# Three kinds of multiplication moved from VectorE to GpSimd in a two-layer hybrid decoder

## The chip, the cores and the metric

The kernel runs on one core of a Trainium2 chip. The metric is the device time of one execution in microseconds (us). The engines are TensorE (PE in the profile, its weight loads PEld), VectorE (DVE), ScalarE (ACT), GpSimd (POOL) and SyncE (SP), whose queue issues the loads of weights. Each engine works through its own queue in order, and semaphores order the engines among each other.

## What is computed

Two layers on an input of 256 positions by 2048 features, float32:

```
h = rmsnorm(x);  z = h @ w_in                      # [q | k | v | u | gate_attn | gate_ssm]
g_attn, g_ssm = sigmoid(z_gates + gate_bias)
y_attn = sliding_window_attention(q, k, v)         # 16 heads, window 128
y_ssm  = glu(gelu(s5_ssm(u)))                      # 64 groups, a scan over the positions
merged = g_attn * (y_attn @ w_attn_branch) + g_ssm * (y_ssm @ w_ssm_branch)
x = x + merged @ w_out
x = x + (silu(h2 @ w_gate) * (h2 @ w_up)) @ w_ffn_out     # h2 = rmsnorm(x)
```

## The kernel before

The layout is transposed: features lie on the 128 partitions and the 256 positions on the free axis. A projection is worked in slabs of 256 output features; a slab is a row of pieces of 512 input rows (four for `w_in` with its 2048 rows, two for the attention branch with its 1024). For accuracy each piece of weights is split in two: ACT casts the high half (`Weights.high`, L106), DVE subtracts to get the low half (`Weights.low`, L121, 128x1024), and PE multiplies both (L295): the high half with 512 columns, the low one with 256. Two accumulators in PSUM rotate, so a slab can begin only when the slab before the last one has been read out. There are four buffers for each of the raw, high and low pieces.

A slab is read out by `whole` (L340): ACT copies one half of the accumulator into a buffer `wh` (tag `t2`, seven rotate; L343), and DVE adds the other half from PSUM (L344). Because the norm's gain is in the input and its root mean square is not, the sum is then multiplied by `rms` (a 128x256 tile repeated over the slab's two halves).

The order is written by hand: a counter ticks once per piece, `later(n, f)` runs `f` in the program n pieces later, and `stages(n, gen)` runs a generator's next step at each further piece. A layer's slabs run in this order: the inputs of the states (u), k and v, q, then eight slabs of the attention branch's gate (`ga`, L898), eight of the attention branch itself (L918), eight of the states' gate (`gs`, L945), the gated linear unit, the states' branch with the merge (L1026, L1027), `w_out`, and the feed-forward part. Beside them run, a few instructions per piece: the attention of eight pairs of heads (`attend`: the score pass L853 on DVE, exponentials on ACT, transposes L874 and products L848, L885 on PE), beside the slabs of q and `ga`; and the scan of the states (`scan`, L768 and L771: two products and four additions per step on DVE, 127 steps a layer), from the slabs of u to the middle of those of `gs`. The scan's end is waited for by PE's read-out of the states (L965).

The gate of the attention branch goes through a sigmoid on ACT in place (L363, from two pieces after the last `ga` slab), and the branch's slabs are multiplied into it (L918). The states' gate goes through its sigmoid on ACT right after its multiplication (L945). `c_matrices` (L925) fills two tiles with zeros on POOL (L929, L930) and has ACT copy into them (L935), three pieces after the last slab of the branch. Otherwise POOL has only memsets and constants.

Of the kernel before, what the change touches and what calls it, by code (L numbers as in the profile page):

```python
# [135 lines left out]
class Clock:  # L136
# [6 lines left out]
    def later(self, n, fn, *args):  # L143
        self.jobs.setdefault(self.now + max(n, 1), []).append((fn, args))

    def stages(self, n, gen, step=1):


        def go():
            if next(gen, "end") != "end":  # L150
                self.later(step, go)

        if n > 0:
            self.later(n, go)
        else:
            go()
# [11 lines left out]
def build(ctx, tc, a, out):  # L168
    nc = tc.nc
    v, s, g, pe = nc.vector, nc.scalar, nc.gpsimd, nc.tensor  # L170
# [16 lines left out]
    def p8(x, shape, dt=F32):  # L187
        return big.tile(shape, dt, name=nm(x), tag="p8", bufs=8)
# [4 lines left out]
    def t2(x, shape=None, dt=F32):  # L193
        return tmp.tile(shape or [P, 2, T], dt, name=nm(x), tag="t2", bufs=7)
# [5 lines left out]
    later, stages = ck.later, ck.stages  # L200
# [107 lines left out]
    def slab(key, rhs, wide):  # L308
        for ps in products(key, rhs, wide):
            pass  # L310
        return ps
# [28 lines left out]
    def whole(ps, x="wh"):  # L340

        t = t2(x)
        s.copy(t, ps[:, :, T:])  # L343
        v.tensor_add(t, t, ps[:, :, :T])  # L344
        return t

    def over(r):
        return r.unsqueeze(1).to_broadcast([P, 2, T])
# [12 lines left out]
    def sigmoid(o, i, **kw):  # L361
        tables("sigmoid_and_others")
        s.activation(o, i, AF.Sigmoid, **kw)  # L363
# [342 lines left out]
    def layer(l, norm):  # L706
        last_layer = l == L - 1
        rms = norm.r
# [44 lines left out]
        for i in range(4):  # L753
            wide = l > 0 or i > 0
            ps = slab((l, "in", 6 + i), norm.rhs, wide)
# [67 lines left out]
        ps = slab((l, "in", 4), norm.rhs, True)  # L823
        stages(1, normed(kt, ps, qkg[:, l, 1:2]))
        ps = slab((l, "in", 5), norm.rhs, True)
# [63 lines left out]
        for i in range(4):  # L889
            ps = slab((l, "in", i), norm.rhs, True)  # L890
# [4 lines left out]
        ga = []  # L895

        def evict_ga(i, ps):
            v.tensor_mul(ga[i // 4][:, 2 * (i % 4) : 2 * (i % 4) + 2, :], whole(ps), over(rms))  # L898

        for i in range(8):  # L900
            if i % 4 == 0:
                ga.append(p8("ga", [P, 8, T]))
            ps = slab((l, "in", 10 + i), norm.rhs, True)
            later(1, evict_ga, i, ps)
# [10 lines left out]

        def evict_ab(i, ps):
            t = ga[i // 4][:, 2 * (i % 4) : 2 * (i % 4) + 2, :]
            v.tensor_mul(t, t, whole(ps))  # L918

        for i in range(8):  # L920
            ps = slab((l, "ab", i), lambda k: ya[k // 4][:, k % 4, :, :], True)
            later(1, evict_ab, i, ps)
# [19 lines left out]

        def evict_gs(i, ps):
            t = whole(ps, "gs")
            v.tensor_mul(t, t, over(rms))  # L945
            for r in range(2):
                sigmoid(gs[i // 4][:, 2 * (i % 4) + r, :], t[:, r, :], bias=gate_b[:, l, 16 + 2 * i + r : 17 + 2 * i + r])

# [49 lines left out]
        for i in range(8):  # L998
            if i % 4 == 0:
                gs.append(p8("gs", [P, 8, T]))  # L1000
            ps = slab((l, "in", 18 + i), norm.rhs, True)
            later(1, evict_gs, i, ps)


        yg, y = hold["yg"], hold["y"]
# [10 lines left out]
        for i in range(4):  # L1016
            ps = slab((l, "glu", i), lambda k: yg[:, 0, k, :, :], True)
# [13 lines left out]
        for i in range(2, 8):  # L1031
            ps = slab((l, "sb", i), lambda k: yg[:, 1, k, :, :], True)
# [10 lines left out]
        def x_tile(i):  # L1043
            return xn[i // 4][:, 2 * (i % 4) : 2 * (i % 4) + 2, :]

        for i in range(8):
            xo = t2("xo")
            nc.sync.dma_start(xo, src[:, 2 * i : 2 * i + 2, :])
            ps = slab((l, "o", i), lambda k: mg[:, k, :, :], True)
            t = x_tile(i)  # L1050
# [27 lines left out]
        for part, nf in enumerate(FPARTS):  # L1078
            hid = [p8("hid", [P, 4, 2, T], F32R) for _ in range(nf // 4)]
            for i in range(nf // 2):  # L1080
                ps = slab((l, "fg", f0 // 2 + i), norm2.rhs, True)
                stages(3 if part == 0 and i == 0 else 1, gate(ps, i))
                ps = slab((l, "fu", f0 // 2 + i), norm2.rhs, True)
# [14 lines left out]
            for i in range(8):  # L1098
# [3 lines left out]
                ps = slab((l, "fo", part, i), hrhs, True)  # L1102
                t = x_tile(i)
# [17 lines left out]
    for l in range(L):  # L1121
        norm = layer(l, norm)
# [61 lines left out]
```

## Time and profile before

| | |
|---|---|
| median of 3 runs | 2625.94 us (2624.06 to 2626.17) |
| the profiled execution | 2625.52 us, its span 2623.70 us |
| mean granted clock of TensorE | 0.997 of full speed |
| PE, DVE, ACT, POOL busy | 99%, 73%, 48%, 1% of the span |

The busy shares are averages over stages that differ, and PE's ends are modelled, so they are read together with the views by stretch, the waits and the chain of work that ended last. That chain is followed back from the last instruction, at each step to what released it or to the instruction before it on its engine.

### The profile page before, as it was taken

The page shows a single profiled execution, that of the slowest core. Times are in us where ns is not written, and L with a number is a line of the kernel's source. Part 1 is how long each engine was busy: PE and PEld are TensorE (multiplying, and loading weights), DVE is VectorE, ACT ScalarE, POOL GpSimd, SP SyncE. Part 2 cuts the span into 40 slices and gives each one's busy share as a digit, 9 for nine tenths or more (in the row PEclk, how much of TensorE's full clock was granted, in tenths as well). Part 3 has the DMA queues.
Part 4 walks back from the last instruction along what each step waited for, and adds up shares of the span by engine and source line. Part 5 has one row for each costly group of instructions (what it writes and reads, how often), then busy time and mean ns, then how long its engine had stood idle before and what let it go on. Part 6 is the DMA issues. An engine that isn't in the chain of part 4 may idle for free.

```text
span 2623.7 us, 40564 instructions
## 1 busy us (share of the span) xinstructions
PE 2586.1 (99%) x15716; PEld 2254.0 (86%) x15716; DVE 1927.0 (73%) x3655; ACT 1267.4 (48%) x1725; POOL 18.9 (1%) x27
## 2 busy tenths in 40 slices
PE   8999899999999999999999999999999999999999
PEld 7878778888888888888888788888888888888888
DVE  8889997866865666566677999887766656665664
ACT  6566546544443444344455675464544334433442
POOL 1000000000000000000000000000000000000000
PEclk9999999999999999999999999999999999999999
DMA  6534554666655565555664445556666556655655
GB/s 220 177 113 145 155 171 157 205 212 194 200 169 193 194 191 178 191 192 186 204 206 148 137 156 171 177 177 211 208 186 190 181 197 191 188 190 185 187 181 171
DMA packets 139825, 477.85 MB, mean 182 GB/s; under 512 B 14960, under 2 KB 25456, under 8 KB 139632
## 3 DMA queue, kind: packets, MB, share of 16 engines
q1 hardware_dynamic: 139488, 475.06, 56.9%
q8 instruction: 123, 2.02, 0.3%
q14 instruction: 70, 0.57, 0.1%
q10 hardware_dynamic: 144, 0.20, 0.0%
HBM read 471.01 MB, written 4.19 MB: 181 GB/s over the span
## 4 chain that ended last, share of the span: by engine, by line
PE 83%; DVE 14%; ACT 1%; issue 1%; DMA 0%; SPq 0%; ACTq 0%; DVEq 0%
PE acc L295 80%; DVE wlo L121 5%; DVE S L771 3%; DVE sc L768 2%; DVE wh L344 1%; PE v L748 1%; PE ys L965 1%; DVE scs L853 1%; DVE ga L918 0%; DMA w<-in_w_in 0%; ACT whi L106 0%; PE acc L323 0%; DVE ga L898 0%; PE bt L673 0%; PE qn L808 0%
## 5 line engine op out<-in xcount | busy, mean ns | idle before, releaser
L106 ACT CAST whi<-w 128x1024 fp32r<-128x1024 f32 (+1 forms) x881 | 911.2, 1047 | 780.3 <-PE acc L295 605.6
L121 DVE TENSOR_TENSOR wlo<-w,whi 128x1024 fp32r<-128x1024 f32 (+1 forms) x881 | 1061.6, 1219 | 217.6 <-ACT whi L106 216.9
L295 PE MATMUL acc<-h,whi 128*128 128x512 f32 x4448 | 1127.3, 395 | 2.5 <-DVE wh L344 1.7
L295 PEld LDWEIGHTS acc<-h,whi 128*128 128x128 f32 x4448 | 801.8, 189 | 158.1 <-issue 9.6
L295 PEld LDWEIGHTS acc<-h,wlo 128*128 128x128 f32 x4448 | 605.2, 190 | 57.5 <-DVE wlo L121 15.4
L295 PE MATMUL acc<-h,wlo 128*128 128x256 f32 x4448 | 622.1, 283 | 8.3 <-DVE wlo L121 8.1
L295 PE MATMUL acc<-hid,whi 128*128 128x512 f32 x1384 | 346.6, 392 | 0.0
L295 PEld LDWEIGHTS acc<-hid,whi 128*128 128x128 f32 x1384 | 249.0, 189 | 44.4
L337 DVE TENSOR_REDUCE j<-acc 128x512 f32<-128x1024 f32 x88 | 107.8, 1224 | 134.0 <-PE acc L295 133.8
L295 PEld LDWEIGHTS acc<-hid,wlo 128*128 128x128 f32 x1384 | 188.8, 191 | 13.4
L295 PE MATMUL acc<-hid,wlo 128*128 128x256 f32 x1384 | 193.0, 283 | 0.0
L1104 DVE TENSOR_TENSOR xn<-xn,acc 128x512 f32<-128x512 f32 x47 | 32.3, 688 | 173.5 <-PE acc L295 173.5
L771 DVE TENSOR_TENSOR S<-S,sc 128x32 f32<-128x32 f32 x1016 | 153.4, 222 | 0.0
L295 PE MATMUL acc<-mg,whi 128*128 128x512 f32 x512 | 128.2, 392 | 0.0
L768 DVE TENSOR_TENSOR sc<-scan_c,S 128x64 f32<-128x64 f32 x508 | 115.7, 269 | 0.0
L295 PEld LDWEIGHTS acc<-mg,whi 128*128 128x128 f32 x512 | 92.1, 189 | 16.4
L295 PE MATMUL acc<-yg,whi 128*128 128x512 f32 x384 | 96.2, 392 | 0.0
L295 PEld LDWEIGHTS acc<-yg,whi 128*128 128x128 f32 x384 | 69.1, 189 | 12.3
L295 PE MATMUL acc<-ya,whi 128*128 128x512 f32 x256 | 67.2, 405 | 9.5 <-DVE wh L344 9.5
L351 ACT CAST hid<-j 128x512 fp32r<-128x512 f32 x44 | 27.4, 623 | 96.9 <-DVE j L1074 96.9
L295 PEld LDWEIGHTS acc<-mg,wlo 128*128 128x128 f32 x512 | 69.9, 190 | 5.0
L295 PE MATMUL acc<-mg,wlo 128*128 128x256 f32 x512 | 71.4, 282 | 0.0
(237 smaller groups left out, 1474.2 us busy)
## 6 DMA issues: line engine op xcount, KB each, us to landing
w<-in_w_fi SPq DMA_DIRECT2D x352, 512.0 KB, 4.3
w<-in_w_in SPq DMA_DIRECT2D x207, 512.0 KB, 3.6
w<-in_w_fo SPq DMA_DIRECT2D x176, 512.0 KB, 4.4
w<-in_w_out SPq DMA_DIRECT2D x64, 512.0 KB, 4.4
w<-in_w_ab SPq DMA_DIRECT2D x32, 512.0 KB, 3.5
w<-in_w_sb SPq DMA_DIRECT2D x32, 512.0 KB, 4.1
w<-in_w_glu SPq DMA_DIRECT2D x16, 512.0 KB, 3.9
x<-in_x SPq DMA_DIRECT2D x8, 256.0 KB, 5.9
```

The costliest lines, as they stand in the source:

```text
L106: self.nc.scalar.copy(part[0][:, f, :], w[:, f, :])
L121: self.nc.vector.tensor_sub(lo[:, f, :], w[:, f, :], hi[:, f, :].bitcast(F32))
L295: pe.matmul(o, w, r, start=start, stop=last and j == m - 1 and lo_part == 1, skip_group_check=True)
L337: v.tensor_reduce(t, ps.rearrange("p s (a t) -> p s t a", a=2), axis=AX.X, op=ALU.add)
L344: v.tensor_add(t, t, ps[:, :, :T])
L351: s.copy(hi, src)
L748: pe.matmul(pss[r][:, c0 : c0 + P], bt[ri][o : o + 64, 2 * q4 + i, :], ur[o : o + 64, 2 * q4 + i, :], start=True, stop=True)
L768: v.tensor_mul(pr, scan_c[:, l, :, :, f], S[:, :, f, c - 1].unsqueeze(1).to_broadcast([P, 2, 2, 16]))
L771: v.tensor_add(S[:, :, f, c], S[:, :, f, c], pr[:, :, r, :])
L853: v.tensor_tensor_reduce(scs[b][:, f, :], scs[b][:, f, :], pv[:, f, :], 1.0, sk[:, b : b + 1], ALU.add, ALU.max, accum_out=mx[:, b, n : n ...
L965: pe.matmul(dst, c[:, ri, pr, :], src, start=bool(odd) and ri == 0, stop=ri == 1, skip_group_check=True)
L1104: v.tensor_add(t, t, ps[:, :, :T])
```

## The change

The multiplications by `rms` of the `ga` and `gs` slabs and the multiplication of the attention branch into `ga` are issued on GpSimd (`g`) in place of VectorE (`v`); the add in `whole` stays on VectorE. `evict_gs` becomes a generator: its two sigmoids are issued one piece after the multiplication, no longer at once. Lines of the changed kernel after L945 lie one line further down.

```diff
         def evict_ga(i, ps):
-            v.tensor_mul(ga[i // 4][:, 2 * (i % 4) : 2 * (i % 4) + 2, :], whole(ps), over(rms))
+            g.tensor_mul(ga[i // 4][:, 2 * (i % 4) : 2 * (i % 4) + 2, :], whole(ps), over(rms))
...
         def evict_ab(i, ps):
             t = ga[i // 4][:, 2 * (i % 4) : 2 * (i % 4) + 2, :]
-            v.tensor_mul(t, t, whole(ps))
+            g.tensor_mul(t, t, whole(ps))
...
         def evict_gs(i, ps):
             t = whole(ps, "gs")
-            v.tensor_mul(t, t, over(rms))
+            g.tensor_mul(t, t, over(rms))
+            yield
             for r in range(2):
                 sigmoid(gs[i // 4][:, 2 * (i % 4) + r, :], t[:, r, :], bias=gate_b[:, l, 16 + 2 * i + r : 17 + 2 * i + r])
...
             ps = slab((l, "in", 18 + i), norm.rhs, True)
-            later(1, evict_gs, i, ps)
+            stages(1, evict_gs(i, ps))
```

## Rows read from the trace of the kernel before

**Rows 1.** The page's first part: busy time, share of the span and instructions of each engine.

```profile
PE 2586.1 (99%) x15716; PEld 2254.0 (86%) x15716; DVE 1927.0 (73%) x3655; ACT 1267.4 (48%) x1725; POOL 18.9 (1%) x27
```

**Rows 2.** Busy time by stretch: the stretch and its length in us, busy us of PE, PEld, DVE, ACT and POOL with their instructions, the granted clock, the share of the DMA engines and GB/s. The first row is the wide stretch 145 to 415; 172 to 276 holds the `ga` slabs of layer 0, 276 to 332 those of its attention branch, 332 to 393 its `gs` slabs up to the scan's end; the last three are of layer 1.

```profile
145.00:415.00 270.00, 254.35 (x1691) 212.29 (x1690) 252.48 (x994) 149.11 (x284) 3.64 (x2) 0.98 0.47 147
172.00:276.00 104.00, 98.48 (x606) 81.06 (x602) 103.14 (x442) 66.75 (x151) 3.64 (x2) 0.98 0.47 145
276.00:332.00 56.00, 49.95 (x266) 42.53 (x267) 55.69 (x214) 26.37 (x38) 0.00 (x0) 0.97 0.50 155
332.00:393.00 61.00, 57.00 (x337) 47.74 (x339) 60.86 (x252) 28.58 (x39) 0.00 (x0) 0.99 0.55 167
1495.00:1559.00 64.00, 63.83 (x413) 54.05 (x414) 62.27 (x250) 46.14 (x106) 1.82 (x1) 0.97 0.49 152
1559.00:1625.00 66.00, 62.97 (x361) 53.93 (x359) 65.62 (x244) 38.73 (x64) 1.81 (x1) 1.00 0.55 169
1625.00:1687.00 62.00, 61.87 (x355) 54.51 (x356) 61.79 (x235) 31.46 (x43) 0.00 (x0) 1.00 0.60 186
```

**Rows 3.** Waits, who for whom: us in total, times, the longest. The first two are PE's from 145 to 415, the last is DVE's from 1470 to 1730 (there is no such wait of DVE from 145 to 415).

```profile
PE acc L295 <- DVE wh L344: 8.0, 7, 2.1
PE acc L295 <- DVE wlo L121: 3.5, 4, 1.6
...
DVE wlo L121 <- ACT whi L106: 1.3, 6, 0.2
```

**Rows 4.** The chain of work that ended last, in order of time, within one slab of the attention branch of layer 0: start, us on the chain, what.

```profile
290.38 0.69 DVE ga L918
291.07 1.14 DVE wlo L121
...
296.00 0.60 DVE wh L344
```

**Rows 5.** The same chain in layer 1, where it is on PE: one row of the `ga` slabs, and the row from the end of the attention branch to the states' read-out.

```profile
1502.06 8.59 PE acc L295 x48
...
1625.13 61.72 PE acc L295 x352
```

**Rows 6.** Busy time of single lines by stretch, the count of their instructions in brackets: two rows for L898, two for L918, two for L945.

```profile
172.00:393.00 221.00, 5.54 (x8) 0.98 0.50 153
1495.00:1559.00 64.00, 3.46 (x5) 0.97 0.49 152
...
172.00:393.00 221.00, 5.53 (x8) 0.98 0.50 153
1559.00:1625.00 66.00, 4.15 (x6) 1.00 0.55 169
...
172.00:393.00 221.00, 2.77 (x4) 0.98 0.50 153
1625.00:1687.00 62.00, 2.77 (x4) 1.00 0.60 186
```

**Rows 7.** DVE's timeline in order, the end of one `ga` slab of layer 0: start, us, engine, line, operation, tiles, shapes.

```profile
248.64 0.68 DVE L344 TENSOR_TENSOR wh<-wh,acc 128x512 f32<-128x512 f32 x1
249.35 0.69 DVE L898 TENSOR_TENSOR ga<-wh,rms 128x512 f32<-128x512 f32 x1
249.96 1.22 DVE L121 TENSOR_TENSOR wlo<-w,whi 128x1024 fp32r<-128x1024 f32 x1
```

**Rows 8.** POOL's timeline: an operation that reads one tile, and two memsets of different widths.

```profile
1.18 0.29 POOL masks.py:199 TENSOR_SCALAR_AFFINE_SELECT ident<-ident 128x128 f32<-128x128 f32 x1
...
7.23 0.95 POOL L679 MEMSET k<- 128x1024 f32 x1
...
1556.12 1.82 POOL L929 MEMSET cb<- 128x2048 f32 x1 [963.72 <-ACT scs L843]
```

**Rows 9.** POOL's timeline: the memset of layer 0 that lies beside the DVE instructions of rows 7; in brackets POOL's idle time before it and what ended it.

```profile
248.49 1.82 POOL L929 MEMSET cb<- 128x2048 f32 x1 [240.30 <-DVE S L771]
```

**Rows 10.** DVE's groups of instructions from 145 to 415, those with an operand in PSUM: count, busy us, mean ns of one, idle time before them.

```profile
L344 DVE TENSOR_TENSOR wh<-wh,acc 128x512 f32<-128x512 f32 x17 | 11.5, 678 | 0.0
L853 DVE CUSTOM_DVE_ANT_0 scs<-scs,sc,params 128x256 f32<-128x256 f32 x14 | 6.7, 477 | 0.0
...
L853 DVE CUSTOM_DVE_ANT_0 scs<-scs,sc,params 128x128 f32<-128x128 f32 x14 | 4.8, 342 | 0.0
...
L344 DVE TENSOR_TENSOR gs<-gs,acc 128x512 f32<-128x512 f32 x6 | 4.1, 680 | 1.2 <-ACT gs L343 1.2
L967 DVE SCALAR_TENSOR_TENSOR y<-u,params,ys 128x256 f32<-128x256 f32 x8 | 3.8, 481 | 9.6 <-PE ys L965 9.6
...
L373 DVE SCALAR_TENSOR_TENSOR rs<-qn,rs 128x512 f32<-128x512 f32 x2 | 1.4, 685 | 1.8 <-ACT rs L370 1.8
```

**Rows 11.** ACT's timeline between the attention branch and the second slab of `gs` in layer 0: a cast of weights, the copies into the zeroed tile, and two pairs of sigmoids; in brackets ACT's idle time before them and what ended it.

```profile
333.70 1.05 ACT L106 CAST whi<-w 128x1024 fp32r<-128x1024 f32 x1 [2.77 <-DVE sc L768]
334.66 2.51 ACT L935 COPY cb<-cc 64x512 f32<-64x512 f32 x4
...
344.30 0.91 ACT L363 ACTIVATE gs<-gs,params 128x256 f32<-128x256 f32 x2 [3.03 <-DVE gs L945]
...
356.37 0.91 ACT L363 ACTIVATE gs<-gs,params 128x256 f32<-128x256 f32 x2 [5.83 <-DVE gs L945]
```

## Prediction

> **What bounds the kernel now.** I read four views. The totals [rows 1] call TensorE (PE) busy for 99% of the span, but the ends of matmuls are modelled, so I ask next what each stretch waits for. The table by stretch [rows 2] shows three stretches of layer 0 (172 to 393 us) and one of layer 1 (1559 to 1625) in which VectorE (DVE) works nearly all the time while PE has idle time: in layer 0, 5.5 + 6.1 + 4.0 = 15.6 us in 221, in layer 1, 3.0 us in 66. The waits [rows 3] say for whom PE waits there: for DVE's add in `whole` (L344), which frees an accumulator, and for the low halves of the weights (L121). The chain [rows 4] runs over DVE alone for pieces at a time, and the moved multiplication (L918) stands in it. So in these stretches DVE sets the pace: a microsecond off its queue is a microsecond off the end, until PE's own pace is reached. Elsewhere the chain is on PE [rows 5]: from 1495 to 1559 (DVE idle for 1.7 us of 64), from 1625 to 1687 (DVE idle for 0.2 of 62, so a little more on DVE would bring it back into the chain), and after 393 and 1687, where DVE has room.
>
> **Where the 48 multiplications lie.** Eight each of L898, L918 and L945 in each layer; the counts by stretch [rows 6] give layer 0 20 in its DVE-bound stretch (8 + 8 + 4). Of layer 1's `ga`, 5 lie in the PE-bound stretch 1495 to 1559 and the other 3 in stretches where the chain is on DVE; 6 of L918 lie on the chain too, so 9 in all; the 2 left of L918 and 4 of L945 lie in the balanced stretch up to 1687. The last 4 of each layer fall where DVE has room and count as nothing; if that cover were gone they would add what the others do.
>
> **What DVE gets back.** From the start of `whole`'s add to that of the multiplication is 0.71 us, from there to the next instruction 0.61, in the order of DVE's queue [rows 7]. Without the multiplication the next instruction can follow the add after 0.61, as others do, so DVE's queue is 0.71 us shorter for each one. If nothing else happened: layer 0, 20 x 0.71 = 14.2 us (less than PE's 15.6 idle, so all of it counts); layer 1, 0.7 for the one `ga` ahead of 1495 and, between 1559 and 1625, no more than PE's idle 3.0 there, 3.7 in all. Sum 17.9 us.
>
> **What POOL needs for one.** No two-input operation on POOL (GpSimd) is in the trace. A memset of 1024 columns takes 0.95 us and one of 2048 takes 1.82 [rows 8]: 0.85 ns a column and 0.08 us before it, 0.52 us for 512 columns. An affine_select of 128 columns, which reads one tile, takes 0.29, so 1.64 ns a column and 0.92 us for 512. A second read at the same step (0.79 ns a column) makes 2.43 ns a column, 1.32 us. Bounds 0.52 and 1.32; the affine_select is the nearest row and lacks one read, so I take 1.1, between it and the upper end.
>
> **What that costs DVE** is the disputed term. Lower end, zero: while POOL filled 2048 columns at 248.49 us, DVE's multiplication at 249.35 took its usual 0.69 us and the subtraction behind it its usual 1.22 [rows 7, 9]. Upper end, the whole of POOL's time. The memset writes one tile and reads nothing, while the moved operation reads two tiles, and so does most of DVE's work here: of the 252.5 us that DVE is busy from 145 to 415 [rows 2], only the groups with an operand in PSUM (the adds of L344 15.6, the score pass L853 11.5, L967 3.8, L373 1.4, together 32.3 us or 13%) read fewer than two from SBUF [rows 10]. So the row with zero is of another kind, and I stay near the upper end: POOL and DVE take turns at reading SBUF, and of POOL's 1.1 us only the 13% beside DVE's PSUM work is free. DVE then loses 0.96 and gets 0.71 back: +0.25 us each.
>
> The Trainium skill states this as a rule ("SBUF — State Buffer", section "Who interferes with whom"): a VectorE instruction with two inputs in SBUF contends with a GpSimd instruction that reads SBUF, not with one that only writes it, and the second to start is blocked until the first is done. By that rule the sum is the forecast's, without it the 17.9 us gain above. The memset row agrees with its second half; no row here shows the first.
>
> **The other edits.** The `yield` in `evict_gs` issues the two sigmoids one piece later on ACT. Today ACT stands before them for 3.0 to 5.8 us with the next casts of weights queued behind [rows 11]; afterwards one cast goes ahead, and the sigmoids wait for POOL, not DVE. DVE waits for casts hardly at all here (1.3 us in all from 1470 to 1730) [rows 3], so I cost it at nothing; should POOL be late by several us, the casts behind would starve DVE (a rival, below). The products themselves are read only in the merge, after all slabs of `gs` and of the gated linear unit. POOL's queue also holds the two memsets of `c_matrices`. The first ran at 248 us [rows 9], early, since nothing was ahead; now they stand behind the last L918 (its DVE stage ends at 332). Add a wait of 1.2 for a subtraction, POOL's 1.1 and 1.8 for the first memset: 332 less 0.7 plus 4.1 is 335.4, where ACT begins its copies into that tile at 334.66 [rows 11]. A delay of 0.8 us, less than ACT's idle time of 2.8 us before the cast ahead of it [rows 11]: nothing, or 0.8 a layer without that room. Layer 1 repeats it. The rotating `wh` buffer is held 1 to 2 us longer; there are seven. No DMA is moved; SP's queue is untouched.
>
> **Sum.** Layer 0: 20 x 0.25 = 5.0. Layer 1: 9 x 0.25 = 2.3 in the chain, 6 x 0.25 = 1.5 in the balanced stretch, and the 5 beside PE (1.25) vanish in DVE's 1.7 idle. Together +8.8 on the profiled run's 2625.52 (span 2623.70 and 1.82 around it; the median of the three runs, 2625.94, lies 0.4 higher): 2634. With POOL's upper price, 1.32, and no overlap at all, each costs 0.61: 35 x 0.61 + (3.05 - 1.7) = 22.7, 2648. With 0.52 each gains 0.26 on the chain's 29: about 2618.
>
> **The rivals.** *Independent engines:* POOL reads beside DVE at no cost. Then the 17.9 us come back: 2607.6; once PE's pace is reached in layer 1 nothing more is to be had. For it: the memset row. Against it: that row reads nothing. *POOL only gets the gaps:* DVE's queue is nearly unbroken in these stretches [rows 2], and POOL may start only beside an operation that needs one SBUF input. Beside the score pass, four steps of 0.34 to 0.47 us in a slab, a multiplication of `ga` costs nothing: 11 x -0.71 = -7.8. Beside the add of the next slab (0.61 to the next start) 0.5 us of POOL's time remains: 14 x -0.2 = -2.8 for L918. For the 8 of `gs` ACT waits at the sigmoid, the casts behind it stop, DVE runs dry, and a round of POOL 1.1 + sigmoids 0.91 + cast 1.05 less 0.71 costs up to 2.35 us: between -1.6 and +18.8. Sum -12 to +8, 2613 to 2634, middle 2624. It turns to a loss when more than about half of the `gs` slabs run dry. *The rival of the other sign* is the first one; its deciding point is a loss of DVE under 0.71 us for each multiplication.
>
> **How the numbers follow.** Taking turns 0.52, since the only overlap shown is of an operation that reads nothing and POOL's likely time is longer than the 0.71 that DVE saves; independent 0.30; gaps 0.18. About 0.2% (5.3 us) is what a measurement of this kernel can tell from no change: faster is below 2620.7, slower above 2631.2. Turns: slower 0.44 (POOL's price over 1.0), same 0.07, faster 0.01. Independent: faster 0.29, same 0.01. Gaps: faster 0.05, same 0.08, slower 0.05. Sums: 0.35, 0.16, 0.49. The range runs from 2605, just under the independent case, to 2648, the upper price; outside I leave 0.15. The likeliest case's own range is 2629 to 2648.
>
> **What would show it.** In the profile after: L898, L918 and L945 on POOL, 48 of them, at 1.0 to 1.2 us each when nothing is beside them. Turns: the DVE instruction behind `whole`'s add, or the one after that, takes about 1 us more than its usual 1.22 or 0.2; DVE's busy time does not fall by 48 x 0.69 = 33 us; PE's idle time before L344 and L121 grows. Independent: DVE's durations as before, DVE's busy time 33 us less, PE's idle time gone. Gaps: POOL's multiplications start 5 us and more after their add, and ACT's idle time before the sigmoids grows. I am wrong if POOL takes under 0.8 us or if DVE's subtractions beside it keep 1.22.

## The result, and the profile after

The changed kernel takes 2638.8 us (median of 4 runs, 2638.63 to 2639.22) against 2625.6 for the kernel before: 13.2 us more, ratio 1.0053, 95% interval 1.0040 to 1.0066. The profiled execution took 2638.63 us, its span 2636.9; TensorE's mean granted clock is 0.997 in it as in that of the kernel before, so in sum the clock isn't what differs. The forecast was 2634 with a range of 2605 to 2648.

The first part of the page after (it answers to [rows 1]):

```profile
PE 2587.1 (98%) x15716; PEld 2253.1 (85%) x15716; DVE 1941.7 (74%) x3607; ACT 1268.1 (48%) x1725; POOL 124.0 (5%) x75
```

DVE issues 48 instructions less, which took 33 us before, and yet is busy for 14.7 us more. So its other instructions have become some 48 us longer, one microsecond for each multiplication. DVE's timeline shows which ones (one slab of the attention branch in layer 0):

```profile
292.72 0.68 DVE L344 TENSOR_TENSOR wh<-wh,acc 128x512 f32<-128x512 f32 x1
293.31 1.22 DVE L121 TENSOR_TENSOR wlo<-w,whi 128x1024 fp32r<-128x1024 f32 x1
294.45 1.55 DVE L768 TENSOR_TENSOR sc<-scan_c,S 128x64 f32<-128x64 f32 x2
295.92 0.60 DVE L771 TENSOR_TENSOR S<-S,sc 128x32 f32<-128x32 f32 x4
296.43 1.22 DVE L121 TENSOR_TENSOR wlo<-w,whi 128x1024 fp32r<-128x1024 f32 x1
```

and POOL's beside it:

```profile
293.54 2.15 POOL L918 TENSOR_TENSOR ga<-ga,wh 128x512 f32<-128x512 f32 x1 [5.34 <-DVE wh L344]
```

POOL takes up its multiplication 0.14 us after DVE's add, while DVE is in its subtraction of two SBUF tiles. That one keeps its 1.22 us. Then DVE's next pair, the scan's two products, takes 1.55 us, where the same pair before the add at 291.85 took 0.45: 1.10 us more, and it ends at 296.0, just after POOL's end at 295.69. So POOL's 2.15 us are 0.99 of waiting for the subtraction's end at 294.53 and 1.16 of its own, and for 1.10 of these DVE stands. Over the whole kernel the scan's products, in the two lists of DVE's groups (count, busy us, mean ns, idle time before them), first the kernel before:

```profile
L768 DVE TENSOR_TENSOR sc<-scan_c,S 128x64 f32<-128x64 f32 x508 | 115.7, 269 | 0.0
```

and after:

```profile
L768 DVE TENSOR_TENSOR sc<-scan_c,S 128x64 f32<-128x64 f32 x508 | 159.3, 354 | 0.0
```

43.6 us more, 40 multiplications at 1.09. The other 8 lie behind the scan's end. One of them shows most plainly whom POOL holds up; POOL's timeline and DVE's:

```profile
400.74 2.21 POOL L945 TENSOR_TENSOR gs<-gs,rms 128x512 f32<-128x512 f32 x1 [11.09 <-DVE gs L344]
```

```profile
400.58 1.22 DVE L121 TENSOR_TENSOR wlo<-w,whi 128x1024 fp32r<-128x1024 f32 x1
401.71 0.87 DVE L968 SCALAR_TENSOR_TENSOR y<-u,params,ys 128x256 f32<-128x256 f32 x2
402.50 1.54 DVE L121 TENSOR_TENSOR wlo<-w,whi 128x1024 fp32r<-128x1024 f32 x1
```

After the subtraction come two instructions with an operand in PSUM (`ys`). They run while POOL works and are not stretched: 0.87 us, where the same pair took 0.90 in the kernel before, at 395.37. Only the next subtraction, with both inputs in SBUF, stands for what is left of POOL's time: 1.54 for 1.22.

By stretch after (columns as in [rows 2]), the three of layer 0, the last one longer because the scan's end has moved, then two of layer 1:

```profile
172.00:276.00 104.00, 98.66 (x602) 80.78 (x598) 103.38 (x421) 63.97 (x146) 15.48 (x7) 0.98 0.45 139
276.00:332.00 56.00, 45.32 (x240) 38.37 (x240) 56.00 (x197) 27.48 (x41) 17.35 (x8) 0.97 0.47 148
332.00:399.00 67.00, 61.33 (x343) 51.28 (x341) 67.00 (x263) 31.23 (x42) 14.53 (x7) 1.00 0.52 164
1495.00:1559.00 64.00, 61.49 (x383) 51.85 (x382) 62.57 (x250) 42.17 (x105) 8.81 (x5) 0.95 0.48 148
...
1625.00:1700.00 75.00, 71.85 (x411) 62.56 (x410) 74.76 (x267) 37.31 (x48) 18.89 (x9) 1.00 0.56 176
```

PE's idle time grew where DVE was busy all along (276 to 332: from 6.1 us to 10.7), and its waits with it (PE's waits from 145 to 425, as in [rows 3]):

```profile
PE acc L295 <- DVE wh L344: 10.6, 7, 2.5
PE acc L295 <- DVE wlo L121: 6.2, 6, 2.3
```

Where in the kernel it was lost is read from PE's read-out of the states, which waits for the end of the scan. Its rows in PE's timeline, before:

```profile
392.14 2.27 PE L965 MATMUL ys<-S,cb 128*32 128x127 f32 x37 [2.06 <-DVE S L771]
...
1687.23 1.95 PE L965 MATMUL ys<-S,cb 128*32 128x127 f32 x64
```

and after, one line further down:

```profile
399.22 2.30 PE L966 MATMUL ys<-S,cb 128*32 128x127 f32 x64 [2.06 <-DVE S L771]
...
1700.02 2.30 PE L966 MATMUL ys<-S,cb 128*32 128x127 f32 x64 [1.60 <-DVE S L771]
```

In layer 0 the loss is 7.1 us, in layer 1 12.8 - 7.1 = 5.7, and behind 1700 nothing more (2636.9 - 1700.0 and 2623.7 - 1687.2 differ by 0.4). In layer 1 PE had not waited for the scan; now it does, for 1.60 us.

### The profile page after: what moved, and what is told of

It reads as the page before. It is cut to its first block, busy times and chain, and to the rows that moved or that the text cites. A ratio compares the mean times of both kernels' runs of the same rounds, so it can differ in the third digit from the quotient of the medians.

```text
span 2636.9 us, 40618 instructions
## 1 busy us (share of the span) xinstructions
PE 2587.1 (98%) x15716; PEld 2253.1 (85%) x15716; DVE 1941.7 (74%) x3607; ACT 1268.1 (48%) x1725; POOL 124.0 (5%) x75
## 4 chain that ended last, share of the span: by engine, by line
PE 79%; DVE 17%; ACT 2%; issue 1%; DMA 0%; POOL 0%; SPq 0%; ACTq 0%; POOLq 0%; DVEq 0%
PE acc L295 77%; DVE wlo L121 6%; DVE sc L768 4%; DVE S L771 3%; DVE wh L344 1%; DVE scs L853 1%; PE v L748 1%; PE ys L966 1%; ACT whi L106 0%; ACT scs L867 0%; PE acc L323 0%; DMA w<-in_w_in 0%; PE bt L673 0%; PE qn L808 0%; ACT h L390 0%
## 5 line engine op out<-in xcount | busy, mean ns | idle before, releaser
L768 DVE TENSOR_TENSOR sc<-scan_c,S 128x64 f32<-128x64 f32 x508 | 159.3, 354 | 0.0
L898 POOL TENSOR_TENSOR ga<-wh,rms 128x512 f32<-128x512 f32 x16 | 35.3, 2205 | 1230.8 <-DVE wh L344 1230.8
L295 PE MATMUL acc<-ya,whi 128*128 128x512 f32 x256 | 67.2, 405 | 14.4 <-DVE wh L344 14.4
```

Of the source, the lines that this page charges most:

```text
L295: pe.matmul(o, w, r, start=start, stop=last and j == m - 1 and lo_part == 1, skip_group_check=True)
L768: v.tensor_mul(pr, scan_c[:, l, :, :, f], S[:, :, f, c - 1].unsqueeze(1).to_broadcast([P, 2, 2, 16]))
L898: g.tensor_mul(ga[i // 4][:, 2 * (i % 4) : 2 * (i % 4) + 2, :], whole(ps), over(rms))
```

## The experiments

The theory: GpSimd and VectorE take turns at reading SBUF; each multiplication holds DVE for POOL's 1.1 us (read from the profile after) and takes 0.71 off its queue, so +0.39 where DVE sets the pace. The rivals: lateness (ACT stands before sigmoids that wait for POOL, with casts of weights behind them), any handing over of work between the engines, and a fixed price per turn. All ratios are to the kernel before, run on the same chip.

**One part at a time.** Each of the three edits alone, the rest as before:

```diff
-            v.tensor_mul(ga[i // 4][:, 2 * (i % 4) : 2 * (i % 4) + 2, :], whole(ps), over(rms))
+            g.tensor_mul(ga[i // 4][:, 2 * (i % 4) : 2 * (i % 4) + 2, :], whole(ps), over(rms))
```

> Only the 16 multiplications of the attention branch's gate (L898) on GpSimd, the rest as before. Theory, taking turns: each holds a DVE instruction that reads two SBUF tiles for 1.1 us and takes 0.71 us off DVE's queue, +0.39 where DVE sets the pace: 8 in layer 0 (3.1), 3 in layer 1 (1.2), the other 5 almost hidden by DVE's 1.7 us of idle time (0.2): +4.5 us, some 2630. Rival, lateness: the loss comes from casts queued on ACT behind the sigmoids of the states' gate, which wait for GpSimd; this part has no such wait and gains what DVE saves, -5 to -8, 2618 to 2621.

Measured 2631.1 against 2625.9, +5.2 us, ratio 1.0023 (1.0014 to 1.0031).

```diff
-            v.tensor_mul(t, t, whole(ps))
+            g.tensor_mul(t, t, whole(ps))
```

> Only the 16 multiplications of the attention branch into its gate (L918) on GpSimd. Taking turns: 8 + 6 on the chain and 2 in the balanced stretch at +0.39 each, +6.2 us, some 2632; DVE's product of the scan beside each one takes about 1.1 us longer. Lateness: nobody waits for these products, so -8 us or so (layer 0 alone 8 x 0.71 = 5.7), 2618.

Measured 2632.0, +6.2 us, 1.0024 (1.0013 to 1.0034).

```diff
-            v.tensor_mul(t, t, over(rms))
+            g.tensor_mul(t, t, over(rms))
+            yield
...
-            later(1, evict_gs, i, ps)
+            stages(1, evict_gs(i, ps))
```

> Only the 16 multiplications of the states' gate (L945) on GpSimd, with the sigmoids a piece later. Taking turns: 4 in each layer before the scan's end at +0.39, +3.1 us, some 2629; the 8 behind it nothing. Lateness: the whole loss of 13 us is here, 2636 or more, and ACT's idle time before L363 grows over the kernel before.

Measured 2628.8, +3.0 us, 1.0012 (1.0003 to 1.0021). All three come out at what turns give (4.5, 6.2, 3.1), none at what lateness gives; together they make 14.4, which agrees with the 13.2 of the whole change within the intervals. ACT's wait before the sigmoids of the states' gate didn't grow over the kernel before. ACT's waits before:

```profile
ACT gs L363 <- DVE gs L945: 59.4, 16, 6.8
```

and after the whole change:

```profile
ACT gs L363 <- POOL gs L945: 50.7, 14, 5.9
```

**Only writing.** POOL's work stays, its reading goes:

```diff
-            g.tensor_mul(ga[i // 4][:, 2 * (i % 4) : 2 * (i % 4) + 2, :], whole(ps), over(rms))
+            whole(ps)
+            g.memset(ga[i // 4][:, 2 * (i % 4) : 2 * (i % 4) + 2, :], 0.5)
...
-            g.tensor_mul(t, t, whole(ps))
+            whole(ps)
+            g.memset(t, 0.5)
...
-            g.tensor_mul(t, t, over(rms))
+            g.memset(t, 0.5)
```

> The changed kernel with each of the 48 multiplications replaced by a memset of the same 128x512 on GpSimd: the multiplications by the rms and by the gate are left out. Taking turns at reading: a memset reads nothing, so no DVE instruction is stretched and DVE's queue is 0.71 us shorter for each: 18 us less than before, some 2608. Rival, any work or handing over between the engines costs DVE: DVE's instructions beside the memsets are stretched by about 0.5 us, 2618 or more, or the time stays near 2638.

Measured 2605.0, 20.8 us less than before, 0.9921 (0.9908 to 0.9935). The memsets of `ga` no longer wait for `whole`, those of `gs` do. POOL's timeline:

```profile
333.33 0.53 POOL L947 MEMSET gs<- 128x512 f32 x1 [48.65 <-DVE gs L344]
```

and DVE's beside it:

```profile
333.19 1.22 DVE L121 TENSOR_TENSOR wlo<-w,whi 128x1024 fp32r<-128x1024 f32 x1
334.33 0.45 DVE L768 TENSOR_TENSOR sc<-scan_c,S 128x64 f32<-128x64 f32 x2
```

A memset of the same width starts inside the subtraction, ends after 0.53 us, and neither is changed. So neither POOL's being busy nor the semaphore between the engines (kept at the `gs` slabs) costs DVE anything; and this is about what the change would have brought if the engines read independently of each other (about, since a memset is shorter than a multiplication, and those of `ga` start without a wait).

**One read in place of two.**

```diff
-            g.tensor_mul(t, t, whole(ps))
+            g.tensor_copy(t, whole(ps))
```

and so for the other two parts; the copy of a `gs` slab goes into one more of the seven rotating `t2` buffers.

> The changed kernel with GpSimd copying one 128x512 tile where it multiplied two: the multiplications by the rms and by the gate are left out, every wait stays. Taking turns for the whole of GpSimd's instruction: a copy reads SBUF too, so each holds DVE for as long as the copy lasts, by the rows of before between 0.52 and 0.92 us; against 0.71 saved that is between -0.2 and +0.2 each, 2618 to 2633, and DVE's product of the scan beside it is stretched by the copy's own duration. Rival, only GpSimd's second operand collides: a copy leaves DVE alone, some 2606.

Measured 2615.5, 10.1 us less than before, 0.9962 (0.9948 to 0.9975). POOL's timeline, then DVE's:

```profile
280.87 1.48 POOL L918 COPY ga<-wh 128x512 f32<-128x512 f32 x1 [5.39 <-DVE wh L344]
```

```profile
280.65 1.22 DVE L121 TENSOR_TENSOR wlo<-w,whi 128x1024 fp32r<-128x1024 f32 x1
281.79 0.86 DVE L768 TENSOR_TENSOR sc<-scan_c,S 128x64 f32<-128x64 f32 x2
```

A copy holds DVE too, for 0.86 - 0.45 = 0.41 us, so it isn't POOL's second operand alone that collides; and the hold follows the length of POOL's instruction: behind the subtraction's end at 281.87 the copy takes 0.48 us, where the multiplication took 1.16. With 0.41 the sum is 35 x (0.41 - 0.71) = -10.5, against the -10.1 measured. The time lies below the expected 2618 to 2633, since a copy is shorter than the rows of before had suggested.

**The price doubled.** The branch's part alone, with a second multiplication behind each, into one more of the `t2` buffers:

```diff
-            v.tensor_mul(t, t, whole(ps))
+            w = whole(ps)
+            g.tensor_mul(t, t, w)
+            g.tensor_mul(t2("scr"), t, w)
```

> As the run with only the branch's multiplications (L918) on GpSimd (2632), each followed by a second multiplication of the same tiles into a scratch tile that nobody reads. Taking turns: DVE is held twice, 1.1 us more for each of the 14 on the chain and the 2 in the balanced stretch, +17 us, some 2649. Rival, one handing over is what costs (a fixed wait for each turn, not GpSimd's duration): the second follows without a new wait on DVE, 2632 to 2636.

Measured 2648.6 against 2625.6, +23.1, 1.0088 (1.0074 to 1.0101): 16.9 us more than the +6.2 with one, 1.06 for each of the 16. DVE's timeline:

```profile
283.03 1.22 DVE L121 TENSOR_TENSOR wlo<-w,whi 128x1024 fp32r<-128x1024 f32 x1
284.17 1.55 DVE L768 TENSOR_TENSOR sc<-scan_c,S 128x64 f32<-128x64 f32 x2
285.64 1.72 DVE L771 TENSOR_TENSOR S<-S,sc 128x32 f32<-128x32 f32 x4
```

The first multiplication holds the products (1.55 for 0.45), then DVE gets an instruction through, and the second one holds the additions (1.72 for 0.60). The price is POOL's duration each time, not a fixed price per turn.

**The yield alone.**

```diff
             v.tensor_mul(t, t, over(rms))
+            yield
...
-            later(1, evict_gs, i, ps)
+            stages(1, evict_gs(i, ps))
```

> The kernel before with nothing but the yield: all multiplications on DVE, the states' gate's sigmoids issued a piece later on ACT. Theory: it costs nothing, 2626 within 1.5. Rival, the moved sigmoids push a cast of weights behind the copy of an accumulator and so are a part of the 3 us of the states' gate: 2628 or more.

Measured 2626.3 against 2625.6, 1.0003 (0.9994 to 1.0012): no difference that can be measured, as costed. It does shorten ACT's wait before the sigmoids. Here, and with the multiplications of `gs` on GpSimd as well (the part alone, above):

```profile
ACT gs L363 <- DVE gs L945: 30.6, 12, 4.4
```

```profile
ACT gs L363 <- POOL gs L945: 51.1, 14, 5.9
```

So GpSimd does come later, by some 20 us of ACT's waiting in all. But the yield took 29 us off that waiting and gained nothing, and the part alone costs no more than turns give: this lateness doesn't reach the end.

**The same multiplication beside work with an operand in PSUM.** Six of the eight `ga` slabs of each layer are read out a piece later, between the scan's steps and the score pass L853, which follows at once:

```diff
+            e = g if i < 6 else v
-            v.tensor_mul(ga[i // 4][:, 2 * (i % 4) : 2 * (i % 4) + 2, :], whole(ps), over(rms))
+            e.tensor_mul(ga[i // 4][:, 2 * (i % 4) : 2 * (i % 4) + 2, :], whole(ps), over(rms))
...
-            later(1, evict_ga, i, ps)
+            if i < 6:
+                jobs = ck.jobs.setdefault(ck.now + 2, [])
+                n = next((n for n, (fn, _) in enumerate(jobs) if fn is not scan), len(jobs))
+                jobs.insert(n, (evict_ga, (i, ps)))
+            else:
+                later(1, evict_ga, i, ps)
```

> Six of the eight slabs of the attention branch's gate in each layer are read out one piece later, straight ahead of the score pass L853, with the multiplication on GpSimd; all else as before. Taking turns only with DVE instructions that read two SBUF tiles: the score pass (1.6 us, an operand in PSUM) hides GpSimd's 1.1, no DVE instruction is stretched, and DVE is 0.71 shorter for each: 6 in layer 0 and 1 or 2 in layer 1 count, -4 to -6, some 2620 to 2622. Rival, any DVE work is held: +0.39 each as in the run with this part alone, 2629 to 2631. Second rival, the later read-out makes PE wait for an accumulator: over 2626 with a longer wait of PE for L344.

Measured 2620.4 against 2625.6, 5.2 us less, 0.9981 (0.9973 to 0.9990): faster than both kernels, by a little. POOL's timeline:

```profile
192.56 1.31 POOL L899 TENSOR_TENSOR ga<-wh,rms 128x512 f32<-128x512 f32 x1 [12.37 <-DVE wh L344]
```

and DVE's:

```profile
191.81 0.68 DVE L344 TENSOR_TENSOR wh<-wh,acc 128x512 f32<-128x512 f32 x1
192.40 0.34 DVE L853 CUSTOM_DVE_ANT_0 scs<-scs,sc,params 128x128 f32<-128x128 f32 x1
...
192.67 0.48 DVE L853 CUSTOM_DVE_ANT_0 scs<-scs,sc,params 128x256 f32<-128x256 f32 x1
...
193.07 0.34 DVE L853 CUSTOM_DVE_ANT_0 scs<-scs,sc,params 128x128 f32<-128x128 f32 x1
...
194.14 1.22 DVE L121 TENSOR_TENSOR wlo<-w,whi 128x1024 fp32r<-128x1024 f32 x1
195.28 0.46 DVE L768 TENSOR_TENSOR sc<-scan_c,S 128x64 f32<-128x64 f32 x2
```

POOL now takes 1.31 us from start to end instead of 2.2, the score pass keeps its 0.34 and 0.48, and the products behind keep 0.46. The same later read-out, with the multiplications on DVE:

```diff
-            e = g if i < 6 else v
+            e = v
```

> As the run with six slabs of the gate read out a piece later beside the score pass (2620.4), but with all multiplications on DVE: only the later read-out is left. Theory: the gain of 5 us is that of GpSimd's hidden multiplications, so this is as before, 2626 within 1.5. Rival: the later read-out itself is the gain, 2620 to 2622.

Measured 2626.8 against 2626.0, 1.0003 (0.9994 to 1.0012). So the gain is not that of the later read-out; it is GpSimd's hidden work.

## Why the prediction came out as it did

*The bound* was read rightly: DVE sets the pace in layer 0 from 172 to 393 us, and what is added to its queue there is added to the end. The loss lies in the stretches named, and none behind the scan's end.

*What DVE gets back* is right: after the change the subtraction follows the add by 0.59 us (292.72 to 293.31), where 0.61 was taken.

*POOL's price*, taken as 1.1 between 0.52 and 1.32, measures 1.1 in the hold of DVE's products and 1.06 by the doubled run. With nothing in its way an instruction lasts 1.31 us in the profile (beside the score pass), not the 1.0 to 1.2 named as a sign; that is the upper price, and some 0.2 of it hold nobody up. The choice above the one-read price was right, but the row it was built on was poor: a copy, which reads one tile too, holds DVE for 0.41 us where the affine_select had suggested 0.92.

*The disputed term* went the forecast's way, and the runs show it: a memset costs DVE nothing, a copy its 0.4, a multiplication its 1.1, two of them twice that, and a multiplication beside the score pass nothing. The Trainium skill's rule ("SBUF — State Buffer", section "Who interferes with whom") is what the traces of this case show, in both halves: two SBUF inputs on DVE collide with a reading GpSimd (1.10 us of standing), not with a writing one (0.45 us as ever).

*One sign of being wrong came true*, and yet turns are what the runs show: DVE's subtractions beside POOL keep their 1.22 us. The prediction named two signs that don't fit each other, this one and, for turns, that the instruction behind the add "or the one after that" is stretched. The sign took POOL to be first. In fact the subtraction is already running when POOL arrives (293.31 and 293.54), so POOL stands, and the instruction after it pays, the scan's products.

*Its size was off.* The term that failed is the one that let 13% of POOL's time fall beside DVE's work in PSUM, as if POOL's turns were spread evenly. They aren't: each starts behind the add, while the subtraction runs, and then meets the scan's products. Nothing is free, so each costs 1.10 - 0.71 = 0.39, not 0.25. With this the forecast's own sum gives 20 x 0.39 = 7.8 for layer 0 (measured 7.1) and 15 x 0.39 = 5.9 for layer 1 (5.7): 13.7 against 13.2.

*The five beside PE's pace* in layer 1 were to vanish in DVE's 1.7 us of idle time. That cover mostly held: DVE's idle time from 1495 to 1559 is still 1.4 us, but PE's grew from 0.2 to 2.5 there, so the stretch is now paced by DVE in part. What the five cost by themselves wasn't measured.

*The other edits* cost nothing that can be measured, as costed: the yield alone comes out 0.0003 above the kernel before, inside its interval. The memsets of `c_matrices` did move behind the last L918; ACT waits for the first of them, for 0.8 us in layer 0:

```profile
340.79 2.54 ACT L935 COPY cb<-cc 64x512 f32<-64x512 f32 x4 [0.79 <-POOL cb L929]
```

as worked out. Whether it reaches the end wasn't tried by itself. The run with the branch's part alone has the same wait (0.8 us in layer 0), and its +6.2 us are what 16 turns give without it (16 x 0.39 = 6.2).

*The rivals.* Independent engines would have given about 2605.0 (the memset run) where 2607.6 was worked out. PE's read-out of the states starts at 379.01 and 1665.89 in that run: the gain is 13.1 us in layer 0, where 14.2 was worked out, and 8.2 in layer 1, where the bound by PE's idle time had allowed 3.7. That bound took PE's busy time as fixed, but it is 2575.6 us there, 10.5 less than before. An estimate of some 7 of these is the clock: before, the granted clock was 0.91 from 180 to 200, 260 to 280, 380 to 400 and 1480 to 1500 us, in part at 1.2 GHz, and in the memset run it is 1.000, 2.4 GHz throughout (4 x 20 x 0.09 = 7.2). How much of the gain in layer 1 is the clock's stays open. Gaps fell too: POOL started 0.14 us after its add and had its turn at the end of one subtraction, not 5 us later.

## What to carry to other kernels

An instruction moved from VectorE to GpSimd leaves VectorE's queue, but if it reads SBUF while VectorE reads two SBUF tiles, the two take turns, and here VectorE's turn of standing is longer (1.1 us) than the work it gave away (0.7). Look up which instruction lies next in VectorE's queue when GpSimd starts: beside one with an operand in PSUM the same multiplication was free: with all eight `ga` slabs of a layer on GpSimd in the old place the kernel lost 5.2 us, with six of them read out one piece later (and two back on VectorE) it gained 5.2. Overlap is worked out from the order of the queues, not from shares of busy time.

## What was not expected of the hardware

GpSimd's duration in the profile holds its waiting for the turn: 2.15 us beside the subtraction, 1.31 beside the score pass, for the same multiplication. In the rows shown the one who was running is not cut short: POOL waited out the subtraction, and DVE's next instruction waited out POOL, even though each of the two products takes 0.27 us by itself and needs 64 columns. A copy on GpSimd, 128x512, holds DVE for 0.41 us, less than half of what a multiplication does and less than the 0.53 us that a memset of that size takes.
